# Hybrid block on one core: the place of the residual's LN1 scale and shift in the down-projection

## Chip, cores and metric

The kernel runs on one core of one Trainium2 chip. The metric is the device time of one execution in microseconds (us), as the median of several executions; lower is better. Times inside an execution are read from one profiled execution and count from the start of its span.

## The reference

One post-norm layer over 512 frames of width 1024, all in float32: two token mixers run side by side (a forgetting attention and a gated delta rule), are gated and projected, and then:

```python
h = _layer_norm(ALPHA * h + mixed @ w_o, ln1_g, ln1_b)
ffn = (jax.nn.silu(h @ w_gate) * (h @ w_up)) @ w_down
return _layer_norm(ALPHA * h + ffn, ln2_g, ln2_b)
```

`w_gate` and `w_up` are 1024x2816, `w_down` is 2816x1024. The change concerns the last two lines: the h that is added in the last one is the output of the first LayerNorm, with its scale `ln1_g` and shift `ln1_b`.

## The kernel before

Float32 products are made from pairs: each operand is split into a rounded part (hi, type fp32r) and the rest (lo), and three matmuls stand for one product. ACT makes hi with a cast, DVE makes lo with a subtraction of two tiles in SBUF.

The residual stands in four tiles `resid[t]` of 128 rows by 1024. After the first LayerNorm's statistics, a tile is only normalized (L1504); scale and shift are applied on the way into the FFN, for the transposed copy that the matmuls read (L1519, L1522), while `resid` itself gets them later, on POOL, by four multiplications and four additions of 128x1024 (L1738 to L1740). For that `ln1_g` and `ln1_b` are loaded, broadcast over 128 partitions, into a tile `bc_ln` (`broadcast_rows`, L1344, issued on SP). As soon as these eight instructions have read it, POOL loads `ln2_g` and `ln2_b` into the same slot (L1741, issued on POOL's own queue).

Ahead of it stands the FFN's gate and up product (L1680 to L1735), whose outcome lies in `f_raw`. Behind it stands the down-projection, `row_gemm` (L1353): for each half of the 1024 output columns it walks over the 22 k tiles of `w_down`, two k tiles at a time. Such a step of two is called a chunk here, by its first k tile: 0, 2, ... 20. For a chunk of the first half:

- `prepare(k0)`, that is `split_f` (L1747), splits two k tiles of `f_raw` into hi (ACT, L1757) and lo (DVE, L1758; the tiles `f_l` and `f_lo`);
- `split_weights` loads 512 KB of `w_down` on SP (L272, tile `wr_d`, three buffers), casts it on ACT (L283, `wh_d`, two buffers) and subtracts on DVE (L285, `wl_d`, two buffers);
- 24 matmuls follow (L1364 to L1366): for each of four row tiles and each of two k tiles `f` hi with `wh_d`, `f` hi with `wl_d` and `f` lo with `wh_d`.

The matmuls, casts and subtractions of this part are placed by a scheduler; `high_priority` in L282 pulls the splits of weights ahead. So DVE makes the `f_l` and `f_lo` of all chunks as early as it can, between the first splits of weights, while the FFN's last matmuls and the first chunks run. SP issues its DMAs in order: a load of `wr_d` waits until the subtraction three chunks before it has read its buffer. At the end of a half `ln2_done` (L1794) adds the sums to `resid` on DVE (L1798) and takes statistics; behind the second half the second LayerNorm's scale and shift follow.

Of the kernel before, what the change touches and what calls it, by code (L numbers as in the profile page):

```python
# [13 lines left out]
ALU = mybir.AluOpType  # L14
# [8 lines left out]
NT = SEQ // P  # L23
# [43 lines left out]
SPLIT_AT = 6  # L67
POOL_BIAS = 1.2
TAIL_AT = 1
ON_POOL = False  # L70

C_QA, C_KA, C_VA, C_F = 0, 512, 1024, 1536
C_QB, C_KB, C_VB, C_A, C_B = 1544, 2568, 3592, 4616, 4624
# [4 lines left out]
def hybrid_block(ctx, tc, x, meta_tokens, ln_in_g, ln_in_b, w_in, b_f, conv_w, a_log, dt_bias,  # L78
                 gdn_norm_w, w_out_a, w_out_b, w_o, ln1_g, ln1_b, w_gate, w_up, w_down,
                 ln2_g, ln2_b, out):  # L80
    nc = tc.nc
# [160 lines left out]
    pe_, act_, dve_, pool_ = (Pinned(e) for e in (nc.tensor, nc.scalar, nc.vector, nc.gpsimd))  # L242

    def ln_stats(t, stats, name, dve, eng, stepped=False, rows=P):
        mv = small.tile([P, 2], F32, tag="bnmv", name=f"mv_{name}{t}")[:rows]
        dve.bn_aggr(mv, stats)
        ve = small.tile([P, 1], F32, tag="bnve", name=f"ve_{name}{t}")[:rows]
        y = small.tile([P, 1], F32, tag="rs_y1", name=f"rsy_{name}{t}")[:rows]
        w = small.tile([P, 1], F32, tag="rs_t1", name=f"rst_{name}{t}")[:rows]

        def steps():
            dve.tensor_scalar(ve, mv[:, 1:2], LN_EPS, 2.0 ** -28, ALU.add, ALU.mult)
            yield
            dve.tensor_scalar(w.bitcast(I32), ve.bitcast(I32), 1, None, ALU.logical_shift_right)
            yield
            dve.tensor_scalar(y.bitcast(I32), w.bitcast(I32), -1, 0xDEB759DF - 2 ** 32, ALU.mult, ALU.add)
            for c in (0.75, 0.1875, 3.0 / 1024):
                yield
                eng.tensor_scalar(w, y, y, ve, ALU.mult, ALU.mult)
                eng.tensor_scalar(y, w, -c, y, ALU.add, ALU.mult)  # L260

        if stepped:
            return mv, y, steps()
        for _ in steps():
            pass
        return mv, y

    loaded = {}

    def load_weights(src, k, n, name):  # L270
        raw = wts.tile([P, 1024], F32, tag="raw", name=f"wr_{name}", bufs=RAW)
        nc.sync.dma_start(raw[:, :k * n].rearrange("p (k n) -> p k n", n=n), src)  # L272
        return raw

    def split_weights(src, k, n, name, alt=None):
        raw = load_weights(src, k, n, name) if name not in loaded else loaded.pop(name)
        (hp, ht), (lp, lt) = alt or ((wts, "hi"), (wts, "lo"))
        nb = 1 if alt else SPLIT
        size = k * n if alt else 1024
        hi = hp.tile([P, size], F32R, tag=ht, name=f"wh_{name}", bufs=nb)  # L280
        lo = lp.tile([P, size], F32R, tag=lt, name=f"wl_{name}", bufs=nb)
        with tc.high_priority():  # L282
            nc.scalar.copy(hi[:, :k * n], raw[:, :k * n])  # L283
            eng = nc.vector
            eng.tensor_sub(lo[:, :k * n], raw[:, :k * n], hi[:, :k * n].bitcast(F32))  # L285
        return (hi[:, :k * n].rearrange("p (k n) -> p k n", n=n),
                lo[:, :k * n].rearrange("p (k n) -> p k n", n=n))
# [305 lines left out]
    heads, groups, busy, convs, fox, scanned = {}, {}, [], [], {}, []  # L593
    RS = pool if ON_POOL else dve
    side = []
# [705 lines left out]
    resid = []  # L1301
# [8 lines left out]
    for ct in range(KT):  # L1310
        parts = []
        g = gbanks(f"po{ct}")
        for j, (w, k) in enumerate(((w_out_a, 4), (w_out_b, 8))):
            last = ct == KT - 1
# [29 lines left out]
    def broadcast_rows(g, b, name, eng):  # L1344
        bcast = fin.tile([P, 2, D], F32, tag="bc", name=f"bc_{name}")
        for i, v in enumerate((g, b)):
            eng.dma_start(bcast[:, i, :], v.broadcast_to([P, D]))
        return bcast
# [104 lines left out]
    def ffn_raw(u):  # L1453
        u["raw1"] = load_weights(ffn_cols(u["w"], 2 * u["p"]), KT, P, f"a{u['j']}")
# [40 lines left out]
    ln1 = {}  # L1495
# [167 lines left out]
    def ffn_finish(u):  # L1663
        p, res, q4 = u["p"], u["res"], u["slots"][6]
        pin(nc.vector.tensor_add(res[:, 1, :256], u["v"], q4))
        if u["j"] % 2 == 0:
            pin(nc.scalar.activation(res[:, 0, :], res[:, 0, :], AF.Silu))  # L1667
            pin(nc.scalar.activation(res[:, 1, :], res[:, 1, :], AF.Silu))
            open_gate[p] = res
        else:  # L1670
            sg = open_gate.pop(p)
            if p:
                pin(nc.vector.tensor_mul(f_raw[(p - 1) // 4][:, (2 * p - 2) % 8:(2 * p) % 8 or 8, :], sg, res))
                return
            pin(nc.vector.tensor_mul(res, sg, res))
# [4 lines left out]
    for j, u in enumerate(units_f):  # L1680
# [17 lines left out]
        p1, t, v = (fin.tile([P, 256], F32, tag="u2", name=f"u{i}_{j}", bufs=5) for i in range(3))  # L1698
# [35 lines left out]
        if j == 0:  # L1734
            ffn_g3(u2, pin, nc.gpsimd)  # L1735
    ffn_finish(units_f[FT - 1])
    bc1 = broadcast_rows(ln1_g, ln1_b, "ln1", nc.sync)
    for t in range(NT):  # L1738
        nc.gpsimd.tensor_mul(resid[t], resid[t], bc1[:, 0, :])
        nc.gpsimd.tensor_add(resid[t], resid[t], bc1[:, 1, :])  # L1740
    bc2 = broadcast_rows(ln2_g, ln2_b, "ln2", nc.gpsimd)  # L1741
    fv = [fin.tile([P, 2, SEQ], F32R, tag=f"v{n}{i}", name=f"f_{n}{i}") for n in "hl" for i in range(7)]
    fv = [t[:, i, :] for t in fv for i in range(2)]
    f_hi += fv[:20]
    lo_tiles, big_lo = {0: fv[20:]}, {}

    def split_f(k0):  # L1747
        if k0 < 2:
            return
        part, at = divmod(k0 - 2, KT)  # L1750
        if part not in lo_tiles:
            t = big.tile([P, KT, SEQ], F32R, tag=("xhi", "xlo")[part - 1], name=f"f_lo{part}")
            big_lo[part] = t
            lo_tiles[part] = [t[:, i, :] for i in range(KT)]
        lo = lo_tiles[part]
        for i in range(2):
            nc.scalar.copy(f_hi[k0 + i], f_raw[part][:, at + i, :])  # L1757
            nc.vector.tensor_sub(lo[at + i], f_raw[part][:, at + i, :], f_hi[k0 + i].bitcast(F32))  # L1758
            f_lo.append(lo[at + i])
# [12 lines left out]

    def ln2_scale(t, cols, mv, eng=dve_):
        sl = resid[t][:, cols]
        eng.scalar_tensor_tensor(sl, sl, mv[:, 0:1], bc2[:, 0, cols], ALU.subtract, ALU.mult)

    def ln2_store(t, cols):
        nc.sync.dma_start(ov[:, t, cols], resid[t][:, cols])

    def ln2_shift(t, cols, r):  # L1780
        sl = resid[t][:, cols]
        dve_.scalar_tensor_tensor(sl, sl, r, bc2[:, 1, cols], ALU.mult, ALU.add)
        ln2_store(t, cols)

    def ln2_shift_slow(t, cols, r):
        sl = resid[t][:, cols]
        act_.activation(sl, sl, AF.Copy, scale=r)
        pool_.tensor_add(sl, sl, bc2[:, 1, cols])
        ln2_store(t, cols)

    H0, H1 = slice(0, 512), slice(512, 1024)
# [2 lines left out]
    def ln2_done(half, t, acc, cols):  # L1794
        at = slice(half * 512 + cols.start, half * 512 + cols.stop)
        sl = resid[t][:, at]
        dve = dve_ if half else nc.vector
        dve.scalar_tensor_tensor(sl, sl, ALPHA, acc[:, cols], ALU.mult, ALU.add)  # L1798
        n = 256 if t == NT - 1 else 512
        for q in range(at.start // n, at.stop // n):  # L1800
            dve.bn_stats(stats2[t][:, q, :], resid[t][:, q * n:(q + 1) * n])
        if half and cols.stop < 512:
            ln2_shift_slow(t - 1, H1, scaled[t - 1])
            ln2_shift(t - 1, H0, scaled[t - 1])
        if half == 0 or cols.stop < 512:
            return
        last = t == NT - 1
        mv, scaled[t], steps = ln_stats(t, stats2[t], "l2_", dve_, dve_ if last else pool_, True)
        if not last:
            for _ in steps:  # L1810
                pass
            for cols in (H1, H0):
                ln2_scale(t, cols, mv)
            if t < NT - 2:
                ln2_shift_slow(t, H1, scaled[t])
                ln2_shift(t, H0, scaled[t])
            return
        nm = small.tile([P, 1], F32, tag="ri", name="nm2")
        act_.activation(nm, mv[:, 0:1], AF.Copy, scale=-1.0)
        pre, mine = (H0, slice(512, 768)), slice(768, 1024)  # L1820
        for cols in pre:
            sl = resid[t][:, cols]
            act_.activation(sl, sl, AF.Identity, bias=nm)
            pool_.tensor_mul(sl, sl, bc2[:, 0, cols])
        for i, _ in enumerate(steps):
            if i == TAIL_AT:
                ln2_scale(t, mine, mv)
        for cols in (mine, *pre):
            ln2_shift(t, cols, scaled[t])

    row_gemm(w_down, FT, f_hi, f_lo, 8, held_d, "d", ln2_done, split_f)


# [23 lines left out]
```

## Time and profile before

| what | value |
|---|---|
| median of 3 runs | 1085.3 us |
| lowest, highest | 1083.38, 1093.4 us |
| span of the profiled execution, first to last instruction | 1082.7 us |
| busy: PE, DVE, ACT, POOL | 999.8, 776.7, 446.0, 413.4 us |

The profile gives the span of its execution and no separate device time for it; the lowest run lies 0.7 us above that span and the median 2.6 us. PE is TensorE (matmuls; its weight loads are PEld), DVE is VectorE, ACT ScalarE, POOL GpSimd, SP the engine that issues most DMAs. A row of a timeline gives start, duration, engine, line, operation, out<-in, and in brackets how long the engine was idle before it and on whom it had waited. Matmul rows overlap (each is shown with some 0.40 us, though the next starts 0.23 us later), so spacing is read from their starts, and a few matmul records are missing.

### The profile page before, as it was taken

To read this page: it belongs to the slowest core of one execution; us is meant where nothing else is said; L and a number is where in the kernel's file an instruction comes from. 1 tells how busy PE (TensorE), PEld (TensorE's weight loads), DVE (VectorE), ACT (ScalarE), POOL (GpSimd) and SP (SyncE) were. 2 spreads that over 40 slices of the span, in tenths; PEclk is the share of its full clock that TensorE was granted. 3 is DMA by queue.
4 is the path that set the end of the run, shared out by engine and by line. 5 is a ranking of instruction groups with operands and counts; after the bars stand their busy time and mean duration, and the time that the engine had idled before them with its cause. 6 is when DMAs were issued, how large, how long until landed. Compare 5 with 4: busy or idle time off the path is not lost.

```text
span 1082.7 us, 17684 instructions
## 1 busy us (share of the span) xinstructions
PE 999.8 (92%) x6765; PEld 894.1 (83%) x6765; DVE 776.7 (72%) x1489; ACT 446.0 (41%) x973; POOL 413.4 (38%) x395
## 2 busy tenths in 40 slices
PE   5988999998899998999999999879999999969995
PEld 4877898888888987877878888779999999848885
DVE  6766689478956996684277556789899899972336
ACT  6345355443553455443352224444444444601121
POOL 6344233414242341323339003674655545450005
PEclk9989999999999999999999999989999999979998
DMA  7252312313231332233334335112342342333322
GB/s 227 79 135 79 84 40 76 87 39 101 68 90 43 100 78 68 74 98 97 98 108 136 107 97 156 40 40 87 109 117 81 115 118 79 117 97 98 97 79 77
DMA packets 162224, 100.61 MB, mean 93 GB/s; under 512 B 18780, under 2 KB 150140, under 8 KB 162140
## 3 DMA queue, kind: packets, MB, share of 16 engines
q1 hardware_dynamic: 161788, 98.39, 32.0%
q8 instruction: 53, 0.87, 0.3%
q0 software_dynamic: 352, 1.10, 0.3%
q14 instruction: 31, 0.25, 0.1%
HBM read 90.90 MB, written 8.57 MB: 92 GB/s over the span
## 4 chain that ended last, share of the span: by engine, by line
PE 48%; DVE 39%; issue 7%; ACT 4%; POOL 1%; DMA 1%; DVEq 0%; SPq 0%; ACTq 0%; POOLq 0%
PE o L240 3%; PE ps_z L207 3%; PE d L1365 3%; PE d L1366 3%; DVE wlo_b L1428 3%; DVE tmp L207 3%; PE d L1364 3%; PE ps_ga L207 3%; PE ps_gb L207 3%; DVE t L207 3%; PE ps_va L207 2%; PE ps_v L207 2%; PE po L1321 2%; PE po L1319 2%; PE po L1320 2%
## 5 line engine op out<-in xcount | busy, mean ns | idle before, releaser
L285 DVE TENSOR_TENSOR wl_d<-wr_d,wh_d 128x1024 fp32r<-128x1024 f32 x18 | 26.4, 1465 | 50.6 <-ACT wh_d L283 50.6
L207 DVE TENSOR_TENSOR tmp<-n,t 34x31 f32<-34x31 f32 (+15 forms) x124 | 55.9, 451 | 1.9
L1482 POOL TENSOR_TENSOR wr_a<-wr_a,sums 128x512 f32<-128x512 f32 x22 | 29.2, 1326 | 66.3 <-DVE wl_a L1428 60.5
L207 DVE TENSOR_TENSOR t<-t,tmp 34x31 f32<-34x31 f32 (+15 forms) x124 | 52.4, 423 | 2.1
L283 ACT CAST wh_d<-wr_d 128x1024 fp32r<-128x1024 f32 x18 | 18.9, 1049 | 81.7 <-PE d L1366 59.8
L1365 PE MATMUL d<-wl_d,f_h 128*128 128x512 f32 (+1 forms) x104 | 40.8, 393 | 12.5 <-DVE wl_d L285 12.5
L240 POOL TENSOR_SCALAR rst_l<-rsy_l,ve_l 128x1 f32<-128x1 f32 x21 | 10.7, 509 | 104.1 <-DVE rsy_l L240 102.7
L1476 POOL TENSOR_TENSOR sums<-wr_a,spare_raw 128x512 f32<-128x512 f32 x11 | 14.7, 1335 | 79.1 <-DMA wr_a<-in_w_gate_dram 68.7
L1364 PE MATMUL d<-wh_d,f_h 128*128 128x512 f32 (+1 forms) x104 | 40.4, 388 | 0.0
L1448 PE MATMUL pa<-v_h,wh_a 128*128 128x256 f32 x160 | 39.3, 279 | 0.0
L1448 PE MATMUL pa<-v_h,wl_a 128*128 128x256 f32 x160 | 39.1, 280 | 0.0
L1365 PEld LDWEIGHTS d<-wl_d,f_h 128*128 128x128 f32 x104 | 20.1, 193 | 17.7 <-DVE wl_d L285 13.4
L207 PE MATMUL ps_v<-x_hi,wh_v 128*128 128x268 f32 x128 | 28.6, 307 | 6.3 <-DVE c_k L207 6.3
L1428 DVE TENSOR_TENSOR wlo_b<-wr_b,whi_b 128x1024 fp32r<-128x1024 f32 x11 | 22.6, 2053 | 16.4 <-ACT whi_b L1427 16.4
L285 DVE TENSOR_TENSOR wl_wo<-wr_wo,wh_wo 128x512 fp32r<-128x512 f32 (+1 forms) x16 | 25.7, 1618 | 10.3 <-ACT wh_wo L283 10.3
L1667 ACT ACTIVATE res<-res 128x512 f32<-128x512 f32 x11 | 7.0, 634 | 62.0 <-DVE res L1728 62.0
L207 PE MATMUL ps_q<-x_hi,wh_q 128*128 128x268 f32 x120 | 27.3, 307 | 5.1 <-DVE y_b L207 5.1
L207 POOL COPY pr<-pr 128x16 f32<-128x16 f32 x16 | 4.6, 289 | 68.7 <-ACT pr L207 68.7
L207 POOL TENSOR_TENSOR wl_ga<-wr_ga,wh_ga 128x512 fp32r<-128x512 f32 x14 | 18.7, 1356 | 31.0 <-ACT wh_ga L207 31.0
L1448 PEld LDWEIGHTS pa<-v_h,wh_a 128*128 128x128 f32 x160 | 30.2, 189 | 0.0
L1448 PEld LDWEIGHTS pa<-v_h,wl_a 128*128 128x128 f32 x160 | 30.0, 188 | 0.0
L283 ACT CAST wh_wo<-wr_wo 128x512 fp32r<-128x512 f32 (+1 forms) x16 | 13.3, 836 | 39.2 <-PE po L1320 23.1
(789 smaller groups left out, 3772.4 us busy)
## 6 DMA issues: line engine op xcount, KB each, us to landing
wr_d<-in_w_down_dram SPq DMA_DIRECT2D x18, 512.0 KB
spare_raw<-in_w_gate_dram SPq DMA_DIRECT2D x11, 512.0 KB
wr_b<-in_w_up_dram SPq DMA_DIRECT2D x11, 512.0 KB
wr_a<-in_w_gate_dram SPq DMA_DIRECT2D x11, 512.0 KB
wr_a<-in_w_up_dram SPq DMA_DIRECT2D x11, 512.0 KB
wr_k<-in_w_in_dram SPq DMA_DIRECT2D x8, 512.0 KB
wr_q<-in_w_in_dram SPq DMA_DIRECT2D x8, 512.0 KB
wr_z<-in_w_in_dram SPq DMA_DIRECT2D x8, 512.0 KB
```

What stands on the lines that cost most here:

```text
L207: ins = fn(*a, **k)
L240: return lambda *a, **k: tc.keep_in_program_order(fn(*a, **k))
L283: nc.scalar.copy(hi[:, :k * n], raw[:, :k * n])
L285: eng.tensor_sub(lo[:, :k * n], raw[:, :k * n], hi[:, :k * n].bitcast(F32))
L1319: nc.tensor.matmul(g[:, j, :], wh[:, i, :], hi[i], start=i == 0, stop=False)
L1320: nc.tensor.matmul(g[:, j, :], wh[:, i, :], lo[i], start=False, stop=False)
L1364: nc.tensor.matmul(acc, ah, wh[:, cols], start=kk == 0, stop=False)
L1365: nc.tensor.matmul(acc, ah, wl[:, cols], start=False, stop=False)
L1366: nc.tensor.matmul(acc, al, wh[:, cols], start=False, stop=kk == ktiles - 1)
L1428: order(eng.tensor_sub(lo, src, hi.bitcast(F32)))
L1448: order(nc.tensor.matmul(dst, a[:, k, :], v[i][:, k, :], start=n == 0, stop=n == 11))
L1482: pin(nc.gpsimd.tensor_sub(v1[:, 1], v1[:, 1], sums[:, 0]))
```

## The change

The broadcast load of `ln1_g` and `ln1_b`, the eight POOL instructions on `resid` and the load of `ln2_g` and `ln2_b` are put into a function, which `split_f` calls at k tile 14 of the first half; ahead of the change they stood in front of the loop. The load of the LN1 rows is tied behind the last load of weights that has been issued by then. The other edits give `bc2` another name.

```diff
-ON_POOL = False
+ON_POOL, AFFINE_AT = False, 14
...
-        nc.sync.dma_start(raw[:, :k * n].rearrange("p (k n) -> p k n", n=n), src)
+        loaded["last"] = nc.sync.dma_start(raw[:, :k * n].rearrange("p (k n) -> p k n", n=n), src)
...
-    bc1 = broadcast_rows(ln1_g, ln1_b, "ln1", nc.sync)
-    for t in range(NT):
-        nc.gpsimd.tensor_mul(resid[t], resid[t], bc1[:, 0, :])
-        nc.gpsimd.tensor_add(resid[t], resid[t], bc1[:, 1, :])
-    bc2 = broadcast_rows(ln2_g, ln2_b, "ln2", nc.gpsimd)
+    ln_rows = {}
+
+    def residual_affine():
+        with tc.issue_after(loaded["last"].ins):
+            bc1 = broadcast_rows(ln1_g, ln1_b, "ln1", nc.sync)
+        for t in range(NT):
+            nc.gpsimd.tensor_mul(resid[t], resid[t], bc1[:, 0, :])
+            nc.gpsimd.tensor_add(resid[t], resid[t], bc1[:, 1, :])
+        ln_rows["ln2"] = broadcast_rows(ln2_g, ln2_b, "ln2", nc.gpsimd)
+
...
     def split_f(k0):
+        if k0 == AFFINE_AT:
+            residual_affine()
```

On SP, at the first loads of `w_down` (`wr_d_4` is chunk 4's), before and after the change; the two rows of `bc_ln` are the LN1 rows:

```order
-L272 DMA wr_d_0_10296<-in_w_down_dram 128x2x512
-L272 DMA wr_d_2_10330<-in_w_down_dram 128x2x512
-L272 DMA wr_d_4_10364<-in_w_down_dram 128x2x512
-L272 DMA wr_d_6_10398<-in_w_down_dram 128x2x512
-L1347 DMA bc_ln_10260<-in_ln_g_dram 128x1024
-L1347 DMA bc_ln_10260<-in_ln_b_dram 128x1024
-L272 DMA wr_d_8_10432<-in_w_down_dram 128x2x512
-L272 DMA wr_d_10_10467<-in_w_down_dram 128x2x512
-L272 DMA wr_d_12_10501<-in_w_down_dram 128x2x512
```

```order
+L272 DMA wr_d_6_10384<-in_w_down_dram 128x2x512
+L272 DMA wr_d_8_10418<-in_w_down_dram 128x2x512
+L272 DMA wr_d_10_10453<-in_w_down_dram 128x2x512
+L272 DMA wr_d_12_10487<-in_w_down_dram 128x2x512
+L1347 DMA bc_ln_10517<-in_ln_g_dram 128x1024
+L1347 DMA bc_ln_10517<-in_ln_b_dram 128x1024
 L272 DMA wr_d_14_10535<-in_w_down_dram 128x2x512
```

The two loads went from behind `wr_d_6` to behind `wr_d_12`, past three loads of weights. Nothing else moved: on PE, DVE, ACT and POOL the same instructions stand in the same order as before (the eight of POOL behind the FFN's last one, L1482). On DVE, at the first splits of `w_down`, this order is the following in the changed kernel, and before with other numbers (`wl_d_2` is the lo part of chunk 2's weights, `f_l` and `f_lo` are lo parts of `f`):

```order
L285 TENSOR_TENSOR wl_d_2_10319<-wr_d_2_10316,wh_d_2_10318 128x1024
L1765 TENSOR_TENSOR f_l_10273<-f_xhi,f_h_10263 128x512 x2
L1765 TENSOR_TENSOR f_lo_10448<-f_xlo,f_h_10264 128x512 x2
L1765 TENSOR_TENSOR f_lo_10448<-f_xlo,f_h_10265 128x512
L285 TENSOR_TENSOR wl_d_4_10353<-wr_d_4_10350,wh_d_4_10352 128x1024
L1765 TENSOR_TENSOR f_lo_10448<-f_xlo,f_h_10265 128x512
L1765 TENSOR_TENSOR f_lo_10448<-f_xlo,f_h_10266 128x512 x2
L1765 TENSOR_TENSOR f_lo_10448<-f_xlo,f_l_10267 128x512 x2
L1765 TENSOR_TENSOR f_lo_10599<-f_ra_7678,f_l_10268 128x512 x2
L285 TENSOR_TENSOR wl_d_6_10387<-wr_d_6_10384,wh_d_6_10386 128x1024
L1765 TENSOR_TENSOR f_lo_10599<-f_ra_7678,f_l_10269 128x512 x2
L285 TENSOR_TENSOR wl_d_8_10421<-wr_d_8_10418,wh_d_8_10420 128x1024
```

On DVE nothing moved here. From `wl_d_8` on DVE has one split of weights per chunk, and nothing else until the end of the half.

## Rows read from the trace of the kernel before

**Rows 1.** The profile page, its first line.

```profile
span 1082.7 us, 17684 instructions
```

**Rows 2.** Chain that ended last, around 937 us: start, us, what.

```profile
937.18 3.35 DVE wl_d L285
...
954.39 3.29 DVE wl_d L285
```

**Rows 3.** Waits, 936 to 970 us: total us, times, longest.

```profile
PE d L1365 <- DVE wl_d L285: 12.5, 2, 11.3
```

**Rows 4.** PE timeline, first half of the down-projection.

```profile
938.94 0.40 PE L1364 MATMUL d<-wh_d,f_h 128*128 128x512 f32 x1
940.59 0.49 PE L1365 MATMUL d<-wl_d,f_h 128*128 128x512 f32 x1 [1.25 <-DVE wl_d L285]
...
946.05 0.40 PE L1364 MATMUL d<-wh_d,f_h 128*128 128x512 f32 x1
957.73 0.79 PE L1365 MATMUL d<-wl_d,f_h 128*128 128x512 f32 x1 [11.28 <-DVE wl_d L285]
...
962.48 0.39 PE L1364 MATMUL d<-wh_d,f_h 128*128 128x512 f32 x1
...
976.47 0.40 PE L1364 MATMUL d<-wh_d,f_h 128*128 128x512 f32 x1
```

**Rows 5.** DVE timeline from 935 us on.

```profile
935.36 0.68 DVE L1758 TENSOR_TENSOR f_l<-f_xhi,f_h 128x512 fp32r<-128x512 f32 x1
...
937.10 3.43 DVE L285 TENSOR_TENSOR wl_d<-wr_d,wh_d 128x1024 fp32r<-128x1024 f32 x1
940.46 2.89 DVE L1758 TENSOR_TENSOR f_l<-f_xhi,f_h 128x512 fp32r<-128x512 f32 x1
...
954.32 3.36 DVE L285 TENSOR_TENSOR wl_d<-wr_d,wh_d 128x1024 fp32r<-128x1024 f32 x1
...
972.15 1.23 DVE L285 TENSOR_TENSOR wl_d<-wr_d,wh_d 128x1024 fp32r<-128x1024 f32 x1 [4.36 <-ACT wh_d L283]
...
1006.74 1.31 DVE L1798 SCALAR_TENSOR_TENSOR resid<-resid,d 128x512 f32<-128x512 f32 x2
...
1057.06 1.41 DVE L240 SCALAR_TENSOR_TENSOR resid<-resid,mv_l,bc_ln 128x512 f32<-128x512 f32 x2
```

**Rows 6.** POOL timeline, 936 to 962 us.

```profile
936.94 5.85 POOL L1739 TENSOR_TENSOR resid<-resid,bc_ln 128x1024 f32<-128x1024 f32 x2 [14.30 <-DMA bc_ln<-in_ln_g_dram]
...
960.20 0.60 POOL L1347 DMA_DIRECT2D bc_ln<-in_ln_g_dram  x1 [0.30 <-POOL resid L1740]
```

**Rows 7.** Tile `bc_ln`: count, duration ns min/median/max, first and last start, forms.

```profile
L1739 POOL TENSOR_TENSOR resid<-resid,bc_ln x4: 2510/2784/3386, 936.9 to 951.1; 128x1024 f32<-128x1024 f32 x4
L1740 POOL TENSOR_TENSOR resid<-resid,bc_ln x4: 2780/2818/3345, 942.8 to 956.6; 128x1024 f32<-128x1024 f32 x4
```

**Rows 8.** Busy us by stretch (x instructions): PE, PEld, DVE, ACT, POOL, granted clock, DMA.

```profile
937.00:945.00 8.00, 6.75 (x30) 5.14 (x29) 8.00 (x4) 3.82 (x7) 8.00 (x3) 1.00 0.26 83
945.00:957.00 12.00, 1.45 (x7) 0.83 (x5) 11.97 (x5) 1.04 (x1) 12.00 (x6) 0.65 0.00 0
...
957.50:962.20 4.70, 4.47 (x11) 3.51 (x12) 4.70 (x6) 0.00 (x0) 3.55 (x3) 0.50 0.48 146
962.50:970.00 7.50, 7.50 (x34) 6.00 (x33) 5.22 (x7) 1.06 (x1) 0.00 (x0) 1.00 0.64 208
```

**Rows 9.** SP timeline, the LN1 rows and chunk 8's load.

```profile
930.47 0.46 SPq L1347 DMA_DIRECT2D bc_ln<-in_ln_g_dram  x1
...
940.56 0.38 SPq L272 DMA_DIRECT2D wr_d<-in_w_down_dram  x1
```

**Rows 10.** DMA issues: KB each, median us to landing.

```profile
bc_ln<-in_ln_b_dram POOLq DMA_DIRECT2D x1, 512.0 KB, 4.9
```

**Rows 11.** ACT timeline, casts of chunks 6 and 10.

```profile
946.25 1.04 ACT L283 CAST wh_d<-wr_d 128x1024 fp32r<-128x1024 f32 x1 [5.43 <-PE d L1366]
...
971.07 1.05 ACT L283 CAST wh_d<-wr_d 128x1024 fp32r<-128x1024 f32 x1 [4.54 <-PE d L1366]
```

More of the change, by code (lines that the diff above doesn't have):

```diff
@@ L1774, in ln2_scale @@
         sl = resid[t][:, cols]
-        eng.scalar_tensor_tensor(sl, sl, mv[:, 0:1], bc2[:, 0, cols], ALU.subtract, ALU.mult)
+        eng.scalar_tensor_tensor(sl, sl, mv[:, 0:1], ln_rows["ln2"][:, 0, cols], ALU.subtract, ALU.mult)
     def ln2_store(t, cols):
@@ L1781, in ln2_shift @@
         sl = resid[t][:, cols]
-        dve_.scalar_tensor_tensor(sl, sl, r, bc2[:, 1, cols], ALU.mult, ALU.add)
+        dve_.scalar_tensor_tensor(sl, sl, r, ln_rows["ln2"][:, 1, cols], ALU.mult, ALU.add)
         ln2_store(t, cols)
@@ L1787, in ln2_shift_slow @@
         act_.activation(sl, sl, AF.Copy, scale=r)
-        pool_.tensor_add(sl, sl, bc2[:, 1, cols])
+        pool_.tensor_add(sl, sl, ln_rows["ln2"][:, 1, cols])
         ln2_store(t, cols)
@@ L1823, in ln2_done @@
             act_.activation(sl, sl, AF.Identity, bias=nm)
-            pool_.tensor_mul(sl, sl, bc2[:, 0, cols])
+            pool_.tensor_mul(sl, sl, ln_rows["ln2"][:, 0, cols])
         for i, _ in enumerate(steps):
```

## The prediction

> **What bounds the kernel now.** I read the chain that ended last first, then the waits, and then the timelines of PE, DVE and POOL where the two agree. Near the start of the down-projection the chain leaves PE and runs over DVE, with splits of weights of 3.3 us [rows 2]; the waits of that stretch say that PE stood for DVE's `wl_d` twice, 12.5 us in all [rows 3]. The PE timeline shows both places: 1.25 us idle in chunk 2 and 11.28 us in chunk 4 [rows 4]. DVE was not idle meanwhile, it was slow: the subtraction of 128x512 that takes 0.68 us at 935 takes 2.89 at 940, and the split of 128x1024 that takes 1.23 us at 972 takes 3.43 and 3.36 at 937 and 954 [rows 5]. The slow stretch begins at 937.10, right after POOL's first instruction on `resid` at 936.94, and POOL's block of eight ends just before 960.20 [rows 6]. In 945 to 957 both DVE and POOL are busy throughout and PE for 1.45 us of 12 [rows 8]. After the long gap PE comes back at half speed: granted clock 0.50 in 957.5 to 962.2, that is the 1.2 GHz level, and 1.00 (2.4 GHz) after that [rows 8]. From there on PE runs without a gap and the splits wait for it, not it for them: ACT's cast of chunk 10 waited for PE, and DVE's split for that cast [rows 5, 11]. So the place where POOL's block lies is bound by DVE, and all other chunks by PE.
>
> **What the change moves.** By the order on SP, only the two loads of the LN1 rows move, from ahead of `wr_d_8` to behind `wr_d_12`. POOL's eight instructions keep their place in POOL's queue, but POOL waited for exactly that load before (14.30 us idle [rows 6]), so a later load is a later block. No instruction is added or removed.
>
> **The gain, step by step.** Spacing first: from the 962.48 matmul to the 976.47 one there are 60 matmuls (half of chunk 4 behind its 12th, chunks 6 and 8), so 13.99/60 = 0.2332 us each, 5.60 us per chunk of 24 [rows 4]. Chunk 2 begins at 938.94; the 962.48 matmul is the 13th of chunk 4, 24 + 12 = 36 starts later. Without a gap it would start at 938.94 + 36 x 0.2332 = 947.33. The loss is 962.48 - 947.33 = 15.15 us. Its parts: the second matmul of chunk 2 starts 1.65 instead of 0.23 us after the first (1.4), the rest of that chunk loses 0.1, the second of chunk 4 starts 11.68 after the first (11.45), and 11 steps at the low clock take 4.75 instead of 2.57 (2.2).
>
> All of it comes back if DVE, alone, keeps ahead of PE. Neighbouring rows of DVE overlap by 0.07 us (937.10 + 3.43 against 940.46 [rows 5]), so a split alone holds the next one up by 1.16 us and a 128x512 subtraction by 0.61. In DVE's order: `wl_d_2` from 937.10 ends at 938.33, and chunk 2 begins at 938.94, 0.6 us to spare. Five subtractions later `wl_d_4` runs from 941.3 to 942.5; chunk 4 would begin at 938.94 + 5.60 = 944.54. Seven more, and `wl_d_6` runs from 946.7 to 948.0 (ACT's cast, which waits for PE to finish chunk 2, starts 0.2 us after chunk 4's first matmul as before, 946.25 against 946.05 [rows 4, 11], so 944.7, and is done at 945.8); chunk 6 begins at 950.14. So PE does not wait, and without a gap I have no reason for the clock to drop: 1.00 is granted in 937 to 945, where the 1.25 us gap lies [rows 8].
>
> **What it costs at the new place.** SP issues a weights load as soon as the split three chunks back is done: 940.56 behind 937.10 + 3.43 [rows 5, 9]. So `wr_d_12` goes out at 948.0, the LN1 scale at about 948.5. It landed 6.47 us after its issue before, at POOL's start (930.47 to 936.94 [rows 6, 9]); a load of the same size took 4.9 on POOL's queue [rows 10]. That puts POOL's start at 953 to 955; I take 955.0, the pattern of loads ahead of it being the same. By then DVE's last `f_lo` is done (949.1). The block lasted 23 us before; eight at the medians of 2.78 and 2.82 us give 22.4 [rows 7], so it ends at 977.4. In it DVE has only the splits of chunks 10 to 16, four of them, 5.6 us apart.
>
> Each can come behind a POOL instruction. The dearest rows are 3.43 us for a split, 2.20 more than alone [rows 5]; the lower end is no delay. Alone, chunk 10's split ends at 972.15 + 1.23 = 973.38 and its chunk begins at 976.47, 3.09 us to spare [rows 4, 5]. With 2.20 lost, 0.9 us are left and PE sees nothing: 0 us, and this spare time is the cover. Even a split that waited a whole longest POOL instruction, 3.39 us [rows 7], would cost PE 0.3 us per chunk, 1.2 us over four. I take 0.
>
> The Trainium skill, "SBUF — State Buffer", section "Who interferes with whom", says that a DVE instruction with two SBUF inputs contends with a GpSimd instruction that reads SBUF, and that whichever is first holds the port for its whole instruction while the other blocks. The rows agree: a 0.68 us subtraction behind a 2.8 us POOL instruction takes 2.89, and not a share of something. By this rule the collision does not go with the move, it finds other victims; one block per split changes nothing in the sum, and the rule names no order for the next in line, which is the third rival.
>
> The rest is covered. SP: the LN1 rows now stand ahead of `wr_d_14`, which waits for chunk 8's split (about 952.6) and is cast 14 us later, against 4.9 to 6.5 us for a load. POOL's own loads of the LN2 rows go out at 977 and land near 982 [rows 10]; DVE reads them first at 1057.06 - 15.15 = 1041.9. `resid` is read at 1006.74 - 15.15 = 991.6 [rows 5], 14 us after POOL's end.
>
> **Sum.** The span of 1082.7 [rows 1] becomes 1067.55. The profile has no device time beside its span; the median lies 2.6 above it, the fastest run 0.7. I carry the difference to the median: 1085.3 - 15.15 = 1070.1 us, 1.4% less.
>
> **Rivals.**
>
> *First rival: two POOL instructions ahead of each split.* If POOL takes the port twice before DVE gets in, a split waits 2.20 + 2.78 = 4.98 us, 1.89 over the spare 3.09; four chunks lose 7.6 us, and the time is 1077.7. Against it: no row of before is longer than one POOL instruction and DVE's own time. For it: those rows come from a stretch in which DVE's next instruction always stood ready.
>
> *Second rival: the block does not move.* POOL's order is unchanged, and if its start depended on something other than that load, nothing would change: 1085.3. Against it stand the 14.30 us that it waited for the load, and SP's order, by which the load cannot go out ahead of chunk 6's split.
>
> *Third rival, slower: POOL keeps DVE out until its block is done.* Chunk 10's split, due at 957.0, would wait until 955.0 + 22.4 = 977.4 and end at 978.6; chunk 10 should begin at 961.34. PE would stand 17.3 us and lose 2.2 to the clock, 19.5, so 4.3 more than is won: 1089.6. At the block's longest, eight of 3.39 us, it would be 1094. It decides from a wait of about 16 us for one split (3.09 spare and 12.95 of stall, with the 2.2 of the clock). Against it: before, DVE got from `wl_d_2` to `wl_d_4`, seven subtractions, inside the block (937.10 to 957.68 [rows 5]). For it: there DVE's pressure was constant, here it comes once in 5.6 us.
>
> **How the numbers follow.** Forecast 0.84, first rival 0.08, second 0.03, third 0.05. A measurement here can tell about 1%, 10.9 us, from no change; the forecast is faster by more than that even if 4 us of it fail. First and second rival and most of the third lie within 1%, 0.14; only the third's dearest end, with a clock that comes back later than before, is slower by more than 1%: 0.02. The range begins at the span of before less the gain, 1067, as the runs may lie closer to their span than the median does, and ends at 1078 with the first rival, which leaves out about 0.1.
>
> **What would show it.** Right: PE's wait for `wl_d` near 940 and 946 is gone and the granted clock is 1.00 throughout the half; the subtractions `f_l` and `f_lo` are all near 0.68 us; POOL's block starts at 953 to 955, behind DVE's last `f_lo`; four splits of weights inside it take up to 3.4 us and PE has no gap there; the last 28 us, the second LayerNorm, are as before. Wrong: a PE wait for `wl_d` in chunks 10 to 16 (first or third rival, told apart by its length), POOL's block still at 937 (second), or a gap of PE at 938 to 950 with POOL idle, which would mean that DVE's list is too long by itself.

## The result and the profile after

| | before | after |
|---|---|---|
| median of 4 runs | 1089.06 us | 1073.46 us |
| lowest, highest | 1083.38, 1093.4 us | 1070.8, 1076.85 us |
| ratio after to before, 95% interval | | 0.985 [0.981, 0.989] |
| span of the profiled execution | 1082.7 us | 1073.1 us |
| chunk 0's first matmul | 933.34 us | 938.99 us |
| from there to the end of the span | 149.36 us | 134.11 us |

The change is 1.5% faster; by the medians 15.6 us, by the interval 12 to 21 us. The two spans differ by 9.6 us only, because the changed kernel's profiled execution reached chunk 0 of the down-projection 5.65 us later. The change has no part in that: POOL's last instruction ahead of its block (L1482) is late by the same 5.65 us already (927.00 against 921.35), before the loads that move are issued in either kernel. So the table has a line that leaves this out: the stretch from chunk 0's first matmul to the end of the span. It fell by 15.25 us. All experiments below are read by it, each from one profiled execution; it agrees to half a microsecond between kernels that should be equal (134.07 to 134.57 below), while whole times differ by some 10 us.

The waits of the changed kernel, 936 to 970 us (waiter <- awaited: total us, times, longest):

```profile
POOL resid L1743 <- DMA bc_ln<-in_ln_g_dram: 31.5, 1, 31.5
ACT wh_d L283 <- PE d L1366: 17.5, 4, 4.5
DVE wl_d L285 <- ACT wh_d L283: 9.2, 3, 4.4
```

PE is in no row as a waiter; its 12.5 us for DVE's `wl_d` [rows 3] are gone. POOL waits 31.5 us for the LN1 rows instead of 14.3 [rows 6]. Its timeline, PE's at the first matmuls of chunks 0, 2 and 4, and SP's:

```profile
938.99 0.40 PE L1364 MATMUL d<-wh_d,rb 128*128 128x512 f32 x1
...
944.58 0.40 PE L1364 MATMUL d<-wh_d,f_h 128*128 128x512 f32 x1
...
950.18 0.40 PE L1364 MATMUL d<-wh_d,f_h 128*128 128x512 f32 x1
```

```profile
959.76 4.75 POOL L1743 TENSOR_TENSOR resid<-resid,bc_ln 128x1024 f32<-128x1024 f32 x2 [31.47 <-DMA bc_ln<-in_ln_g_dram]
...
975.89 5.76 POOL L1744 TENSOR_TENSOR resid<-resid,bc_ln 128x1024 f32<-128x1024 f32 x2
981.95 0.60 POOL L1347 DMA_DIRECT2D bc_ln<-in_ln_g_dram  x1 [0.30 <-POOL resid L1744]
```

```profile
953.74 0.37 SPq L272 DMA_DIRECT2D wr_d<-in_w_down_dram  x1
954.20 0.42 SPq L1347 DMA_DIRECT2D bc_ln<-in_ln_g_dram  x1
```

The chunks follow each other every 5.60 us, with no gap where before had 1.25 and 11.28 us [rows 4]. On DVE the list of small subtractions now runs alone, and the splits inside POOL's block are the only slow rows:

```profile
941.00 0.68 DVE L1765 TENSOR_TENSOR f_l<-f_xhi,f_h 128x512 fp32r<-128x512 f32 x1
...
942.74 1.22 DVE L285 TENSOR_TENSOR wl_d<-wr_d,wh_d 128x1024 fp32r<-128x1024 f32 x1
943.88 1.29 DVE L1765 TENSOR_TENSOR f_l<-f_xhi,f_h 128x512 fp32r<-128x512 f32 x2
...
947.01 1.22 DVE L285 TENSOR_TENSOR wl_d<-wr_d,wh_d 128x1024 fp32r<-128x1024 f32 x1
...
952.49 1.22 DVE L285 TENSOR_TENSOR wl_d<-wr_d,wh_d 128x1024 fp32r<-128x1024 f32 x1
...
962.67 2.92 DVE L285 TENSOR_TENSOR wl_d<-wr_d,wh_d 128x1024 fp32r<-128x1024 f32 x1 [4.37 <-ACT wh_d L283]
968.27 3.03 DVE L285 TENSOR_TENSOR wl_d<-wr_d,wh_d 128x1024 fp32r<-128x1024 f32 x1 [2.68 <-ACT wh_d L283]
973.84 3.17 DVE L285 TENSOR_TENSOR wl_d<-wr_d,wh_d 128x1024 fp32r<-128x1024 f32 x1 [2.54 <-ACT wh_d L283]
979.40 3.33 DVE L285 TENSOR_TENSOR wl_d<-wr_d,wh_d 128x1024 fp32r<-128x1024 f32 x1 [2.39 <-ACT wh_d L283]
```

The stretches, in the columns of [rows 8]:

```profile
937.00:945.00 8.00, 8.00 (x45) 6.87 (x44) 8.00 (x14) 8.00 (x16) 0.00 (x0) 1.00 0.23 79
945.00:957.00 12.00, 12.00 (x53) 9.63 (x53) 9.84 (x15) 3.56 (x5) 0.00 (x0) 1.00 0.46 124
957.00:970.00 13.00, 13.00 (x57) 10.47 (x56) 5.88 (x3) 2.14 (x3) 10.24 (x4) 1.00 0.48 169
970.00:980.00 10.00, 10.00 (x45) 8.10 (x44) 5.07 (x3) 2.10 (x2) 10.00 (x5) 1.00 0.34 101
```

PE (first busy number behind the comma) fills every stretch at a granted clock of 1.00 (the third number from the end), and 1.00 is what 939 to 1000.5 shows as a whole. The 12 us of 945 to 957 had held 1.45 us of PE before, and the half clock followed [rows 8].

### The profile page after: what moved, and what is told of

It reads as the page before. It is cut to its first block, busy times and chain, and to the rows that moved or that the text cites. A ratio compares the mean times of both kernels' runs of the same rounds, so it can differ in the third digit from the quotient of the medians.

```text
span 1073.1 us, 17685 instructions
## 1 busy us (share of the span) xinstructions
PE 1001.0 (93%) x6765; PEld 895.4 (83%) x6765; DVE 766.6 (71%) x1489; ACT 445.7 (42%) x973; POOL 412.0 (38%) x395
## 4 chain that ended last, share of the span: by engine, by line
PE 49%; DVE 37%; issue 6%; ACT 4%; DMA 2%; POOL 1%; DVEq 0%; SPq 0%; ACTq 0%; POOLq 0%
PE d L1366 3%; PE d L1364 3%; PE d L1365 3%; PE ps_z L207 3%; DVE wlo_b L1428 3%; DVE tmp L207 3%; PE ps_ga L207 3%; PE ps_gb L207 3%; DVE t L207 3%; PE ps_va L207 3%; PE po L1321 2%; PE po L1319 2%; PE po L1320 2%; PE ps_v L207 2%; PE o L240 2%
## 5 line engine op out<-in xcount | busy, mean ns | idle before, releaser
L285 DVE TENSOR_TENSOR wl_d<-wr_d,wh_d 128x1024 fp32r<-128x1024 f32 x18 | 29.6, 1643 | 45.2 <-ACT wh_d L283 45.2
L1482 POOL TENSOR_TENSOR wr_a<-wr_a,sums 128x512 f32<-128x512 f32 x22 | 29.2, 1325 | 66.4 <-DVE wl_a L1428 66.3
L1365 PE MATMUL d<-wl_d,f_h 128*128 128x512 f32 (+1 forms) x104 | 39.7, 381 | 0.0
L1448 PE MATMUL px<-v_h,rb 128*128 128x256 f32 x176 | 25.5, 289 | 2.9 <-ACT v_h L240 2.9
```

Source lines behind the costliest of these rows:

```text
L1365: nc.tensor.matmul(acc, ah, wl[:, cols], start=False, stop=False)
L1448: order(nc.tensor.matmul(dst, a[:, k, :], v[i][:, k, :], start=n == 0, stop=n == 11))
L1482: pin(nc.gpsimd.tensor_sub(v1[:, 1], v1[:, 1], sums[:, 0]))
```

## The experiments

Two theories could explain the result: POOL's block had held up DVE's list (the prediction's), or the two loads of the LN1 rows, ahead of `wr_d_8`, had held up weights. Eight kernels tell these apart and then ask how the collision works and where the block may stand. The measure is the stretch from chunk 0's first matmul to the end. In e2 an added line shifts the line numbers of the matmuls by one, so its first is an L1365, at 940.63. For e2 and e5 POOL's start is that of the first whole-tile instruction, behind the one-column copies. The ratios are to runs of before taken with each group (medians 1090.37 us for e1 to e4, 1092.62 for e5 to e8).

| kernel | POOL's start, us after chunk 0's first matmul | stretch, us |
|---|---|---|
| before | 3.60 | 149.36 |
| e3, 16 half instructions, old place | 3.94 | 149.67 |
| e4, called at k tile 10 | 11.15 | 141.91 |
| e7, called at 12 | 15.07 | 134.17 |
| after (14) | 20.77 | 134.11 |
| e8, called at 20 | 36.55 | 134.07 |
| e2, rows loaded early, block held | 19.30 | 134.57 |
| e1, block cut to 16 columns, old place | 4.48 | 134.27 |
| e6, block cut to 16 columns, new place | 20.79 | 134.18 |
| e5, fills in place of the block, old place | 6.92 | 134.37 |

**e1: the block cut down at its old place.**

```diff
-        nc.gpsimd.tensor_mul(resid[t], resid[t], bc1[:, 0, :])
-        nc.gpsimd.tensor_add(resid[t], resid[t], bc1[:, 1, :])
+        nc.gpsimd.tensor_mul(resid[t][:, :16], resid[t][:, :16], bc1[:, 0, :16])
+        nc.gpsimd.tensor_add(resid[t][:, :16], resid[t][:, :16], bc1[:, 1, :16])
```

> The kernel before, with the eight POOL instructions cut to 16 of 1024 columns (the rest of the residual keeps no LN1 scale and shift); all loads stand where they stood. Measure: the stretch from the first matmul of chunk 0 of the down-projection to the end of the span, 149.4 us before and 134.1 after the change. Theory (POOL's block in DVE's way): the stretch falls to about 134, no PE wait for wl_d, DVE's 128x512 subtractions at 0.68 us. Rival (the moved loads: the LN1 rows stood ahead of wr_d_8 and held weights up): the stretch stays near 149. Ratio to before: theory 0.985, rival 1.0.

Measured: 134.27 us, ratio to before 0.985 [0.983, 0.987]. POOL's timeline, and DVE's right behind POOL's start:

```profile
945.51 2.55 POOL L1739 TENSOR_TENSOR resid<-resid,bc_ln 128x16 f32<-128x16 f32 x4 [15.18 <-DMA bc_ln<-in_ln_g_dram]
```

```profile
945.92 1.33 DVE L1758 TENSOR_TENSOR f_l<-f_xhi,f_h 128x512 fp32r<-128x512 f32 x2
947.29 1.95 DVE L1758 TENSOR_TENSOR f_lo<-f_xlo,f_h 128x512 fp32r<-128x512 f32 x3
```

About 0.65 us each, with the loads where they had been. The whole gain comes with the block's work gone, so the order of the loads has no part in it that the stretch shows.

**e2: the loads at the old place, the block held.** The changed kernel; the load of the LN1 rows goes back in front of the loop, and POOL's block begins behind a copy from the raw weights of chunk 12:

```diff
+        loaded["raw"] = raw
...
+    bc1 = broadcast_rows(ln1_g, ln1_b, "ln1", nc.sync)
...
-        with tc.issue_after(loaded["last"].ins):
-            bc1 = broadcast_rows(ln1_g, ln1_b, "ln1", nc.sync)
...
+        pin(nc.gpsimd.tensor_copy(hold, loaded["raw"][:, :1]))
...
```

> The changed kernel with the load of the LN1 rows back at its old place on SP (ahead of wr_d_8), while POOL's eight instructions are held by a copy of one column of the landed wr_d_12. Theory (only the block's place counts): stretch 134 as after the change, POOL's block starts some 15 us or more after the first matmul of chunk 0, no PE wait for wl_d. Rival (the order of the loads brings the gain): stretch near 149.

Measured: 134.57 us, ratio 0.985 [0.982, 0.988], no PE wait for `wl_d`. POOL's timeline:

```profile
959.34 0.64 POOL L1743 COPY hold<-wr_d 128x1 f32<-128x1 f32 x1 [29.36 <-DMA wr_d<-in_w_down_dram]
959.93 2.40 POOL L1745 TENSOR_TENSOR resid<-resid,bc_ln 128x1024 f32<-128x1024 f32 x1
```

The same gain to 0.5 us from the other side: the loads early and the block late. The loads' rival falls. The first instruction, which met no subtraction of DVE, also shows what one of the eight takes alone: 2.40 us.

**e3: sixteen instructions of half the width, old place.**

```diff
-        nc.gpsimd.tensor_mul(resid[t], resid[t], bc1[:, 0, :])
-        nc.gpsimd.tensor_add(resid[t], resid[t], bc1[:, 1, :])
+        for sl in (slice(0, 512), slice(512, 1024)):
+            nc.gpsimd.tensor_mul(resid[t][:, sl], resid[t][:, sl], bc1[:, 0, sl])
+            nc.gpsimd.tensor_add(resid[t][:, sl], resid[t][:, sl], bc1[:, 1, sl])
```

> The kernel before, with each of the eight POOL instructions cut into two of 512 columns, at the old place. Theory (each engine holds the port for one whole instruction, they take turns, and the sum of both engines' work up to chunk 6's split is what counts): DVE's 128x512 subtraction takes about 1.8 us in the block instead of 2.89 (0.61 alone and the 1.2 of a half POOL instruction), the single gap of 11.3 us becomes two, ahead of chunk 4 (about 6) and of chunk 6 (6 to 9), and the stretch stays near 149 (147 to 152). Rival (the two share the port in proportion, whatever the length of an instruction): 2.89 us stays, and the gap ahead of chunk 4 stays 11 us. A third view (shorter POOL instructions cure it): stretch under 143.

Measured: 149.67 us, ratio 1.000 [0.997, 1.004]. DVE and PE:

```profile
965.01 2.28 DVE L285 TENSOR_TENSOR wl_d<-wr_d,wh_d 128x1024 fp32r<-128x1024 f32 x1
967.21 1.76 DVE L1759 TENSOR_TENSOR f_lo<-f_ra,f_l 128x512 fp32r<-128x512 f32 x1
```

```profile
953.36 0.79 PE L1365 MATMUL d<-wl_d,f_h 128*128 128x512 f32 x1 [4.13 <-DVE wl_d L285]
967.34 0.79 PE L1365 MATMUL d<-wl_d,f_h 128*128 128x512 f32 x1 [5.48 <-DVE wl_d L285]
```

The stretches right behind PE's two waits, in the columns of [rows 8]:

```profile
953.30:958.00 4.70, 4.64 (x11) 3.67 (x12) 4.70 (x4) 0.00 (x0) 4.70 (x4) 0.50 0.40 112
967.30:971.00 3.70, 3.66 (x9) 2.89 (x10) 3.70 (x3) 0.00 (x0) 3.40 (x3) 0.50 0.45 142
```

The 128x512 subtraction takes 1.76 us instead of 2.89 [rows 5]: without its own 0.68 it waits 1.08 us instead of 2.21. A half POOL instruction takes 1.3 us elsewhere in the profile and a whole one 2.40 alone (e2), so the wait is one POOL instruction less 0.2 us, and halves with it. The two do not share in proportion. This is also what the page that the prediction named states, "SBUF — State Buffer" of the Trainium skill, "Who interferes with whom": the port is held for a whole instruction. The trace agrees but for those 0.2 us. Yet the time is that of before: the gaps of 1.25 and 11.28 us became 4.13 and 5.48 us. Both gaps are shorter than I had expected (about 6, and 6 to 9), so the stretch came out as expected partly by luck; the half clock, paid twice, makes up for them. POOL gets a turn behind every subtraction until its work is done, so ahead of `wl_d_6` DVE's list still waits for nearly all of it: that split ends 29.7 us after chunk 0's first matmul here (965.01 + 2.28 - 937.63), 32.0 before (964.11 + 1.22 - 933.34, by the row below). The 2.3 us between them are lost again, because PE pays the half clock behind both gaps: 14 matmul steps each take 6.01 us (from 953.36) and 5.86 us (from 967.34) instead of 3.27, so 2.7 and 2.6 us, against 2.2 once.

```profile
964.11 1.22 DVE L285 TENSOR_TENSOR wl_d<-wr_d,wh_d 128x1024 fp32r<-128x1024 f32 x1
```

**e4: called at k tile 10.** `AFFINE_AT = 10`; the rows are loaded behind `wr_d_8`.

> The changed kernel with the call at k tile 10 instead of 14: the rows' load goes out behind wr_d_8, so right behind wl_d_2, and POOL's block starts about 12 us after the first matmul of chunk 0 instead of 21. Theory (what counts is whether the block meets DVE's list of f_lo): it meets the last five or six f_lo ahead of wl_d_6, which then comes some 10 us late: PE waits 7 to 12 us ahead of chunk 6, stretch 143 to 149. Rival (any place behind the loop's first loads will do): stretch 134.

Measured: 141.91 us, ratio 0.988 [0.984, 0.993]. DVE, POOL and PE:

```profile
950.59 2.76 DVE L1765 TENSOR_TENSOR f_lo<-f_ra,f_l 128x512 fp32r<-128x512 f32 x1
...
956.08 3.36 DVE L285 TENSOR_TENSOR wl_d<-wr_d,wh_d 128x1024 fp32r<-128x1024 f32 x1
```

```profile
949.44 6.17 POOL L1743 TENSOR_TENSOR resid<-resid,bc_ln 128x1024 f32<-128x1024 f32 x2 [21.84 <-DMA bc_ln<-in_ln_g_dram]
```

```profile
959.49 0.79 PE L1365 MATMUL d<-wl_d,f_h 128*128 128x512 f32 x1 [4.00 <-DVE wl_d L285]
...
968.38 0.49 PE L1365 MATMUL d<-wl_d,f_h 128*128 128x512 f32 x1 [0.71 <-DVE wl_d L285]
```

Half the loss is back, so not any later place will do. The size was missed (141.91 us against 143 to 149): I had expected five or six subtractions in the block ahead of `wl_d_6`, and DVE had got so far that it met two and the split itself. PE's gaps were 4.00 and 0.71 us, not 7 to 12. From matmul start to matmul start they cost 4.2 and 0.9 us, and the half clock behind the first of them 2.4 more (worked out at the end), 7.5 of the 7.8 us.

**e5: fills instead of the block, old place.** Two one-column copies wait for the rows, then

```diff
-        nc.gpsimd.tensor_mul(resid[t], resid[t], bc1[:, 0, :])
-        nc.gpsimd.tensor_add(resid[t], resid[t], bc1[:, 1, :])
+        for _ in range(6):
+            pin(nc.gpsimd.memset(resid[t], 1.0))
```

> The kernel before, with the eight POOL instructions replaced by 24 fills of 128x1024 on the same tiles, which read nothing from SBUF (the residual is lost), after two copies of one column that wait for the LN1 rows; some 23 us of POOL at the old place, by the 0.95 us of a fill elsewhere in the profile. View A (what collides is the reading of POOL and of DVE): DVE's subtractions stay at 0.68 us, no PE gap, stretch 134 to 135. View B (any work of POOL on SBUF slows DVE): DVE's 128x512 subtraction takes about 1.5 us (0.61 and a fill of 0.95), PE waits ahead of chunks 4 and 6, stretch 140 to 149.

Measured: 134.37 us, ratio 0.983 [0.980, 0.986]. POOL and DVE:

```profile
943.75 0.96 POOL L1743 MEMSET resid<- 128x1024 f32 x1
...
946.69 21.88 POOL L1743 MEMSET resid<- 128x1024 f32 x22
```

```profile
947.82 1.29 DVE L1761 TENSOR_TENSOR f_lo<-f_xlo,f_l 128x512 fp32r<-128x512 f32 x2
...
950.36 1.22 DVE L285 TENSOR_TENSOR wl_d<-wr_d,wh_d 128x1024 fp32r<-128x1024 f32 x1
```

From 943.75 to 968.57 POOL writes 24 tiles of the block's size, over all of DVE's list but its first three subtractions, and DVE loses nothing. So it is POOL's reading that collides with DVE's subtractions of two SBUF tiles, not its writing alone or its being busy. This is what the Trainium skill states in "SBUF — State Buffer", "Who interferes with whom" (two SBUF inputs on DVE against a GpSimd instruction that reads, not one that only writes); the trace agrees, with 0.65 us against 2.89.

**e6: the block cut down at its new place** (e1's edit in the changed kernel).

> The changed kernel with the eight POOL instructions cut to 16 of 1024 columns (the rest of the residual keeps no LN1 scale and shift). Theory (at its new place the block is hidden whole): stretch as after the change, 134.1, within 0.6 us. Rival (the splits that come 1.7 to 2.1 us late there cost PE something): stretch lower by 1 us or more.

Measured: 134.18 us against 134.11 with the whole block; the ratio to before, 0.981 [0.971, 0.991], is too wide to add to this. The block at its new place costs nothing that the stretch can show. POOL:

```profile
952.41 0.76 POOL L1743 TENSOR_TENSOR resid<-resid,bc_ln 128x16 f32<-128x16 f32 x4 [31.49 <-DMA bc_ln<-in_ln_g_dram]
```

Four of these small instructions take 0.76 us here, where DVE has no subtraction, and 2.55 us in e1, beside DVE's list. So the waiting goes both ways: there POOL's instructions stood behind DVE's.

**e7 and e8: called at k tiles 12 and 20.**

> The changed kernel with the call at k tile 12: the rows go out behind wr_d_10, right after wl_d_4, and POOL's block starts some 15.5 us after chunk 0's first matmul, when DVE has two f_lo left and wl_d_6 is done. Theory: nothing on PE's way meets it, stretch 134 to 135, against 141.9 with the call at 10 and 149.4 before. Rival (each place earlier than 14 costs its share): about 138.

> The changed kernel with the call at k tile 20, the last chunk: the rows go out behind wr_d_18, POOL's block starts some 36 us after chunk 0's first matmul and ends near 59, while DVE begins to read the residual at 58.2 (997.2 - 939.0 in the changed kernel). Theory: the first two tiles are done by then, the last addition is awaited for up to 1.5 us, the stretch is 134 to 136. Rival (DVE's late read holds PE's banks and the second half starts late): 138 or more.

Measured: 134.17 us at 12 (ratio 0.980 [0.972, 0.988]) and 134.07 at 20 (0.985 [0.982, 0.988]). DVE at 12, and POOL and DVE at 20:

```profile
953.17 3.50 DVE L1765 TENSOR_TENSOR f_lo<-f_ra,f_l 128x512 fp32r<-128x512 f32 x2
956.61 3.39 DVE L285 TENSOR_TENSOR wl_d<-wr_d,wh_d 128x1024 fp32r<-128x1024 f32 x1
```

```profile
993.93 5.77 POOL L1744 TENSOR_TENSOR resid<-resid,bc_ln 128x1024 f32<-128x1024 f32 x2
```

```profile
998.32 2.46 DVE L285 TENSOR_TENSOR wl_d<-wr_d,wh_d 128x1024 fp32r<-128x1024 f32 x1 [3.26 <-ACT wh_d L283]
1000.71 1.27 DVE L1805 SCALAR_TENSOR_TENSOR resid<-resid,d 128x512 f32<-128x512 f32 x2
```

At 12 the block meets only the end of DVE's list, behind `wl_d_6`, and the splits' spare time covers it. At 20 it ends at 999.70, ahead of DVE's first read of the residual at 1000.71. I had allowed for a wait of up to 1.5 us: that read comes 59.48 us after chunk 0's first matmul, against 58.23 in the changed kernel (997.22 - 938.99), so 1.25 us late, because the split ahead of it stood behind the block's last addition and took 2.46 us. The stretch does not show it. From 12 to 20 the place makes no difference to the time; none of these versions is better than the change.

## Why the prediction was right

- *The bound before: DVE, held up by POOL's block.* Right, and shown by e1 (block gone, gain there), e2 (block moved, loads not) and e5 (POOL busy without reading).
- *The gain of 15.15 us.* The stretch gave 15.25, the medians 15.6. All four parts (two gaps, the rest of chunk 2, the half clock) came back, since the clock stays at 1.00. That the medians agree so closely is partly luck, as their interval is 12 to 21 us; the stretch is the test. Behind it, from POOL's first instruction of the second LayerNorm to the end, nothing changed: 25.4 us in both (from 1057.25 and 1047.72).
- *DVE alone keeps ahead of PE.* `wl_d_4` and `wl_d_6` were forecast to start 8.0 and 13.4 us after chunk 0's first matmul (941.3 and 946.7 less 933.34); they started 8.02 and 13.50 us after it.
- *The new place.* The rows were to be issued 15.2 us after that matmul and were at 15.21; POOL was to start at 21.7 by the pattern of before or 20 by POOL's own loads, and did at 20.77. The block ended 42.7 us after it, forecast 44.1: it began earlier, and took 21.9 us instead of 22.4, as I had used medians of instructions that nearly all had let a subtraction in (2.78 and 2.82 us against 2.40 alone in e2).
- *No cost of four late splits.* They took 2.92 to 3.33 us, under the dearest row of before, 3.43, and left PE alone; without the block (e6) the stretch is no shorter, 134.18 against 134.11.
- *The rivals.* First (two POOL instructions ahead of one split) and third (DVE kept out until the block ends): no split in any run took longer than 3.43 us, less than two POOL instructions of 2.40 us, so in these runs DVE came next whenever one POOL instruction ended. Second (the block does not move): it moved by 17 us. The loads as a cause had not been among the rivals; e1 and e2 exclude it.
- *The time.* 1073.46 us against 1070.1. The gain is the forecast one; the base moved. The median of before had been 1085.3 from three runs and is 1089.06 with a fourth at 1092.82; the same gain taken from that is 1073.9.

What stays open is why PE runs at the half clock for a longer or a shorter time ahead of the down-projection (below).

## What to carry to other kernels

When DVE's rows of one shape take several times their usual duration while POOL works, look at POOL's list at that minute: an elementwise block there can be free by its own engine's idle time and still cost PE, through DVE. (Shown here for DVE's subtractions of two SBUF tiles and POOL instructions that read SBUF; fills on POOL cost nothing.) Move such a block to where DVE has one short instruction per period with spare time behind it, and check the spare time against one whole POOL instruction. Cutting the block into smaller instructions did not help: e3 made each wait shorter and twice as many of them.

## What the runs showed of the hardware that was not expected

- While both had work ready, the two engines took turns: one POOL instruction, one subtraction of DVE, in before (eight and eight inside the block), e3 (sixteen and sixteen) and e4. That a subtraction never waited for two POOL instructions in a row is what the first rival had doubted.
- PE's granted clock fell to 0.50, the 1.2 GHz level, behind gaps of 4.00 (e4), 4.13 and 5.48 us (e3), as behind the 11.28 us of before, and not behind 0.71 (e4) and 1.25 us (before). In e4 twelve matmul steps took 5.22 us (959.49 to 964.71), 2.4 more than at full clock, so the shorter gap cost as much on top as the long one did (2.2). The stretches of e4, of which the first holds the half clock and its end, the second the gap of 0.71 us:

```profile
959.40:966.60 7.20, 7.11 (x21) 5.65 (x22) 7.20 (x4) 0.00 (x0) 7.20 (x3) 0.64 0.24 73
966.60:970.00 3.40, 2.69 (x12) 1.89 (x11) 3.18 (x2) 1.04 (x1) 3.40 (x2) 1.00 0.11 21
970.00:975.00 5.00, 5.00 (x23) 4.01 (x22) 1.67 (x1) 0.96 (x1) 4.69 (x4) 1.00 0.61 196
```

- The first matmul of chunk 0, ahead of which the ten kernels differ only in the two loads of the LN1 rows, issued some 3 us before it in five of them, came between 931.62 (e6) and 941.23 us (e8) in their ten profiled executions, 9.6 us apart: nearly two thirds of what the change is worth, and a reason to read a local change by a local stretch. The difference goes with the clock: ahead of that matmul PE was granted 0.50 for 41.0 us in e6, 47.8 in before, 54.6 in the changed kernel and 61.4 in e8, and over the ten executions the first matmul comes 0.5 us later for each such microsecond (correlation 0.97). The whole times of before go the same way, from 1079.87 us at a mean granted clock of 0.975 to 1093.48 us at 0.962. Why the half clock lasts longer in one execution than in another is not shown.
